# Orders of work at three places of a two-layer encoder kernel: the start, the scan scores, the entry of the odd layer

## The chip, the cores and the metric

The kernel runs on one core of a Trainium2 chip. The metric is the device time of one execution in microseconds (us); lower is better. The time before is the median of three runs, 1917.02 us (1916.12 to 1919.83). The engines are named as in the profile: PE is TensorE, PEld its weight load, DVE is VectorE, ACT is ScalarE, POOL is GpSimd, and SP issues transfers only.

## The reference

The input x has 256 positions (T) of 2048 channels, batch 1, fp32, and there are two layers. Layer 0 is even: one input projection feeds an SSD scan (centred width-5 convolution, chunks of 128, both directions) and a neighbourhood attention, and both go through one output projection. Layer 1 is odd: a convolution module with a GLU, a width-31 convolution and a layer norm. Behind each layer a gate adds a projected per-layer input p[i].

```python
def even_mixer(hn, w_in, ...):
    u = hn @ w_in
    z, xbc, dt_raw, q, k, v, g = jnp.split(u, ...)
    y_ssd = ssd_branch(z, xbc, dt_raw, ...)
    y_na = neighbourhood_attention(q, k, v, rpb) * jax.nn.silu(g)
    return jnp.concatenate([y_ssd, y_na], axis=-1) @ w_out

def conv_module(hn, w_in, dw_w, dw_b, ln_w, ln_b, w_out):
    a, a_gate, g = jnp.split(hn @ w_in, 3, axis=-1)
    v = a * jax.nn.sigmoid(a_gate)
    v = depthwise_conv(v, dw_w, dw_b)
    v = layernorm(v, ln_w, ln_b)
    v = jax.nn.silu(v) * jax.nn.silu(g)
    return v @ w_out

def per_layer_embedding(h, p_i, norm_w, w_gate, w_proj):
    gate = jax.nn.sigmoid(rmsnorm(h, norm_w) @ w_gate)
    return gate * (p_i @ w_proj)

h = x
for i in range(DEPTH):
    h = h + (even_mixer if i % 2 == 0 else conv_module)(rmsnorm(h, ...), ...)
    h = h + per_layer_embedding(h, p[i], ...)
return rmsnorm(h, final_norm_w)
```

In the scan of one group of four heads and one chunk, the scores are (C Bt) times exp(sum of decays) times dt; the kernel calls this product mT.

## The kernel before

**Projections.** Every fp32 projection is done in fp32r: each operand is split into a high part (a copy in fp32r) and a low part (the rest), and three matmuls per tile are summed: high by high, low by high, high by low. `proj` (L277-279) keeps the weights stationary and gives channels by positions; `proj_rows` (L305-307) keeps the activations stationary and gives positions by channels.

**Weights.** The class `Weights` cuts all weights into jobs of 512 KB, in the order in which they are used: two k tiles of 128 rows by 512 columns. For each job SP issues the load into `raw` (L96), ACT makes the high part `whi` (L99), and DVE, or POOL where a table says so, makes the low part `wlo` (L101). There are four buffers for raw and four for the parts. `fill(upto)` emits jobs up to a number, with high priority; `take()` hands the next job to a projection and keeps `AHEAD` = 3 jobs emitted ahead of it.

**Order.** PE runs in the order in which the program is written (`manual_schedule` for PE). On the other engines a scheduler orders the instructions; `tc.high_priority()` puts those inside it ahead of others that are ready. Small pieces of work are generators in the list `bg`: `pump(n)` takes n steps, and a projection calls it between two jobs. `wait(n)` is n empty steps, `drain()` runs all that is left.

**Normalization.** `TokNorm.feed(c)` squares a column block of h on ACT with a sum (L339, one instruction for each half a of the 256 positions); behind the fourth block DVE reduces the sums (L343, L344) and POOL takes the power -1/2 (L345), which gives `rh`. `scaled_blocks` multiplies h by it into `xs` (L418: a=0 on DVE, a=1 on POOL). `transposed` transposes xs on PE into `htp` (L407, two k tiles by four 128x128 transposes a step) and splits that with the norm weight into `ahi` on ACT (L319) and `alo` on DVE (L320), the operands of the next projection.

**The start.** ACT issues p[0] and four loads of x, one for each 512 columns of h (512 KB); POOL issues the first part of `vecs` (all small vectors); three weights are filled. p[0] is transposed and split (`load_p`, L317 for its low part), then the four blocks of h are squared, then four projections of p[0] run (`proj_rows`, four jobs). Their results are copied from PSUM into `ppb` (L432, a=0 on DVE, a=1 on ACT) and stored by POOL to DRAM as `pp0` for the gate. Then xs, two steps of transposes (`START_PAIRS` = 2) and the first big projection, `acc_b0`, of 512 columns. The other part of `vecs` (560 KB) is loaded by SP behind that projection's fill (L523).

**The scan.** Each group has PE build `seg`, the sums of decays, for both chunks (L588); ACT takes the Exp into mT (L593), and DVE multiplies it by dt (L594) and by the C B products (L595). A few jobs later PE multiplies mT with x into `ya` (L607). Between these, ACT and DVE do the width-5 convolution of the next channels: ACT the first tap and the Silu (L505 and L511), DVE four further taps (L509).

**The entry of the odd layer.** The gate of layer 0 (`gate`, with DVE at L765 and L766) adds to h and squares it. Behind it `load_p(1, ...)` issues the load of p[1], its two steps (`ptp`, L393, and split) run at once, then four `proj_rows` with p[1], copied by ACT (L784), then `scaled_blocks` into tiles of the pool `sg`, two steps of transposes, and the first GLU projection.

```python
    for c in range(NB):
        norm.feed(c)
...
    scaled_blocks(norm, xs)
    xn = []
    bg.append(transposed(xs, "ev_norm_w", xn))
    pump(START_PAIRS)
    acc_b0 = proj(LazyList(xn, KT), 512)
```

Of the kernel before, what the change touches and what calls it, by code (L numbers as in the profile page):

```python
# [44 lines left out]
START_PAIRS = 2  # L45
NB = D // 512
# [25 lines left out]
class Weights:  # L72


    def __init__(self, tc, pools, jobs):
# [6 lines left out]
        self.taken = 0  # L82

    def fill(self, upto):
        with self.tc.high_priority():
            while self.emitted < min(upto, len(self.jobs)):
                self.emit()

    def emit(self):
# [6 lines left out]
        nc.sync.dma_start(  # L96
            raw,
            w[k0 * P:(k0 + nk) * P, c0:c0 + ncols].rearrange("(k p) c -> p k c", p=P))
        nc.scalar.activation(hi, raw, AF.Copy)  # L99
        eng = nc.gpsimd if low(i) else nc.vector  # L100
        eng.tensor_sub(lo, raw, hi.bitcast(F32))  # L101
# [10 lines left out]
def trunk(ctx, tc, t, out, dbg=None):  # L112
# [201 lines left out]
    def split(hi, lo, src, scale=None, eng=None):  # L314
        if scale is None:
            nc.scalar.activation(hi, src, AF.Copy)
            (eng or nc.vector).tensor_sub(lo, src, hi.bitcast(F32))  # L317
        else:
            nc.scalar.activation(hi, src, AF.Copy, scale=scale)  # L319
            nc.vector.scalar_tensor_tensor(lo, src, scale, hi.bitcast(F32), op0=ALU.mult, op1=ALU.subtract)  # L320

    def operand(src, scale=None, where=None, eng=None):
        hi = (where or actp).tile([P, T], F32R, name="ahi", tag="ahi")
        lo = (where or actp).tile([P, T], F32R, name="alo", tag="alo")
        split(hi, lo, src, scale, eng)
# [3 lines left out]
    class TokNorm:  # L329


        def __init__(self):
            self.n, self.rstd = 0, None
# [45 lines left out]
    def load_p(i, pl_pool, pt=None):  # L379
# [6 lines left out]
        def steps():  # L386
          with tc.high_priority():
            for k in range(2):
# [5 lines left out]
                split(ph, pl, ps[:, :T])  # L394
                res.append((ph, pl))
                yield
# [15 lines left out]
    def scaled_blocks(norm, xs):  # L412

        with tc.high_priority():
            for c in range(NB):
                for a in range(2):
                    eng = nc.gpsimd if a else nc.vector
                    eng.tensor_scalar(xs[c][a], h[c][:, a, :], norm.rstd[:, a:a + 1], None, op0=ALU.mult)  # L418
# [4 lines left out]
    for _ in steps:  # L423
        pass
    norm = TokNorm()
    for c in range(NB):
        norm.feed(c)
    for c in range(NB):
        ppb = sp.tile([P, 2, 512], F32, name="ppb", tag="ppb")

        def ev_pp(a, acc):
            (nc.scalar.copy if a else nc.vector.tensor_copy)(ppb[:, a, :], acc)  # L432
        proj_rows(pk, ev_pp)
        nc.gpsimd.dma_start(pp_dram[c], ppb)
    xs = [[sp.tile([P, 512], F32, name="xs", tag="xs", bufs=2 * NB) for _ in range(2)] for _ in range(NB)]
    scaled_blocks(norm, xs)
    xn = []
    bg.append(transposed(xs, "ev_norm_w", xn))
    pump(START_PAIRS)
# [522 lines left out]
```

## Time and profile before

| | us |
|---|---|
| median of three runs | 1917.02 |
| the profiled execution, its own time | 1919.01 |
| its span in the trace | 1917.3 |
| mean granted PE clock over the span | 0.987 |
| loads of weights and inputs | 333.11 MB read, 176 GB/s over the span |

The first part of the profile's page gives the busy time of each engine, its fourth part the chain of work that ended last, by engine. A view by stretches gives the busy time of each engine between two points of time, and a list of waits says which operation on PE stood idle for which operation of another engine: its rows read "waiter <- releaser: sum of idle us, times, longest". A row of the timeline is the start of an operation (us from the span's start), its duration, engine, line, operation, tile out<-in, shapes, how many alike follow each other, and in brackets the idle time ahead and what ended it.

### The profile page before, as it was taken

To read this page: it belongs to the slowest core of one execution; us is meant where nothing else is said; L and a number is where in the kernel's file an instruction comes from. 1 tells how busy PE (TensorE), PEld (TensorE's weight loads), DVE (VectorE), ACT (ScalarE), POOL (GpSimd) and SP (SyncE) were. 2 spreads that over 40 slices of the span, in tenths; PEclk is the share of its full clock that TensorE was granted. 3 is DMA by queue.
4 is the path that set the end of the run, shared out by engine and by line. 5 is a ranking of instruction groups with operands and counts; after the bars stand their busy time and mean duration, and the time that the engine had idled before them with its cause. 6 is when DMAs were issued, how large, how long until landed. Compare 5 with 4: busy or idle time off the path is not lost.

```text
span 1917.3 us, 31565 instructions
## 1 busy us (share of the span) xinstructions
PE 1871.3 (98%) x12436; PEld 1723.2 (90%) x12436; DVE 1293.8 (67%) x2119; ACT 951.0 (50%) x1305; POOL 652.6 (34%) x393
## 2 busy tenths in 40 slices
PE   7999999999999999999999999999999999999997
PEld 5999898899999999888887999999999999888885
DVE  4778765664656566665555598888889959765564
ACT  4555554644444455544454544444445447544553
POOL 2002866640000000000000498888888855200011
PEclk8999999999999999999999999999999999999998
DMA  7656445456666666565555476666666655566553
GB/s 250 176 168 185 132 132 154 131 147 182 176 186 165 193 167 191 180 224 188 187 185 166 132 215 183 185 180 180 191 181 184 186 156 165 186 204 203 186 181 117
DMA packets 191189, 339.37 MB, mean 177 GB/s; under 512 B 25376, under 2 KB 34080, under 8 KB 190912
## 3 DMA queue, kind: packets, MB, share of 16 engines
q1 hardware_dynamic: 188480, 331.70, 58.0%
q10 hardware_dynamic: 1936, 3.41, 0.5%
q0 software_dynamic: 624, 2.24, 0.3%
q8 instruction: 97, 1.59, 0.3%
q14 instruction: 52, 0.43, 0.1%
HBM read 333.11 MB, written 4.19 MB: 176 GB/s over the span
## 4 chain that ended last, share of the span: by engine, by line
PE 89%; DVE 5%; issue 2%; DMA 1%; ACT 1%; POOL 1%; ACTq 0%; POOLq 0%; DVEq 0%; SPq 0%
PE acc L278 17%; PE acc L277 17%; PE acc L279 17%; PE acc L305 12%; PE acc L307 12%; PE acc L306 11%; DVE wlo L101 2%; ACT whi L99 1%; DVE xsg L509 1%; PE ya L607 1%; PE htp L407 1%; DVE vc L856 1%; PE seg L588 0%; DMA raw<-in_ev_w_in_dram 0%; DMA h<-in_x_dram 0%
## 5 line engine op out<-in xcount | busy, mean ns | idle before, releaser
L99 ACT ACTIVATE whi<-raw 128x1024 fp32r<-128x1024 f32 (+1 forms) x633 | 656.3, 1037 | 772.3 <-PE acc L278 374.0
L101 DVE TENSOR_TENSOR wlo<-raw,whi 128x1024 fp32r<-128x1024 f32 (+1 forms) x465 | 577.9, 1244 | 434.7 <-ACT whi L99 431.4
L277 PE MATMUL acc<-ahi,whi 128*128 128x256 f32 (+1 forms) x2832 | 806.6, 285 | 1.7 <-ACT ahi L319 1.7
L278 PE MATMUL acc<-alo,whi 128*128 128x256 f32 (+1 forms) x2832 | 803.2, 284 | 3.4 <-DVE alo L320 3.3
L279 PE MATMUL acc<-ahi,wlo 128*128 128x256 f32 (+1 forms) x2832 | 803.0, 284 | 2.0 <-DVE wlo L101 2.0
L278 PEld LDWEIGHTS acc<-alo,whi 128*128 128x128 f32 (+1 forms) x2832 | 543.4, 192 | 5.4 <-DVE alo L320 4.6
L277 PEld LDWEIGHTS acc<-ahi,whi 128*128 128x128 f32 (+1 forms) x2832 | 543.3, 192 | 3.4 <-ACT ahi L319 2.2
L279 PEld LDWEIGHTS acc<-ahi,wlo 128*128 128x128 f32 (+1 forms) x2832 | 543.3, 192 | 2.6 <-DVE wlo L101 2.6
L101 POOL TENSOR_TENSOR wlo<-raw,whi 128x1024 fp32r<-128x1024 f32 (+1 forms) x168 | 385.4, 2302 | 80.0 <-ACT whi L99 77.8
L305 PE MATMUL acc<-whi,ahi 128*128 128x512 f32 x1024 | 405.8, 396 | 2.5 <-DVE q4l L317 2.5
L307 PE MATMUL acc<-whi,alo 128*128 128x512 f32 x1024 | 402.5, 393 | 1.0 <-DVE alo L317 1.0
L306 PE MATMUL acc<-wlo,ahi 128*128 128x512 f32 x1024 | 402.2, 393 | 0.0
L822 DVE SCALAR_TENSOR_TENSOR cacc<-vc,vecs,cacc 128x249 f32<-128x249 f32 (+14 forms) x960 | 376.9, 472 | 8.1 <-ACT cacc L819 5.3
L345 POOL TENSOR_TENSOR rh<-rh,nhalf 128x2 f32<-128x2 f32 x5 | 3.5, 696 | 830.8 <-DVE rh L344 830.7
L307 PEld LDWEIGHTS acc<-whi,alo 128*128 128x128 f32 x1024 | 193.4, 189 | 44.3 <-DVE alo L317 1.4
L305 PEld LDWEIGHTS acc<-whi,ahi 128*128 128x128 f32 x1024 | 193.8, 189 | 43.6 <-DVE q4l L317 2.8
L306 PEld LDWEIGHTS acc<-wlo,ahi 128*128 128x128 f32 x1024 | 193.7, 189 | 40.7
L535 POOL TENSOR_SCALAR_AFFINE_SELECT dm<-dt_tok 128x512 f32<-128x512 f32 x32 | 32.3, 1013 | 140.2 <-DVE dt_tok L484 128.9
L319 ACT ACTIVATE ahi<-htp,vecs 128x256 fp32r<-128x256 f32 x64 | 29.3, 466 | 34.8 <-DVE alo L320 34.8
L809 DVE TENSOR_TENSOR vc<-acc,sg 128x512 f32<-128x512 f32 x16 | 11.1, 691 | 49.3 <-PE acc L279 49.0
L320 DVE SCALAR_TENSOR_TENSOR alo<-htp,vecs,ahi 128x256 fp32r<-128x256 f32 x64 | 30.3, 480 | 15.2 <-ACT ahi L319 15.2
L535 POOL TENSOR_SCALAR_AFFINE_SELECT segr<-ah 128x512 fp32r<-128x512 f32 x32 | 35.5, 1109 | 10.5 <-PE seg L588 10.2
(207 smaller groups left out, 1182.7 us busy)
## 6 DMA issues: line engine op xcount, KB each, us to landing
raw<-in_ev_w_in_dram SPq DMA_DIRECT2D x225, 512.0 KB, 3.7
raw<-in_od_w_in_dram SPq DMA_DIRECT2D x176, 512.0 KB, 4.3
raw<-in_ev_w_out_dram SPq DMA_DIRECT2D x64, 512.0 KB, 4.0
raw<-in_ple_w_gate_dram SPq DMA_DIRECT2D x64, 512.0 KB, 4.0
raw<-in_od_w_out_dram SPq DMA_DIRECT2D x64, 512.0 KB, 4.7
raw<-in_od_w_in_dram SPq DMA_DIRECT2D x32, 256.0 KB, 2.8
raw<-in_ple_w_proj_dram SPq DMA_DIRECT2D x8, 512.0 KB, 4.9
braw<-in_ev_rpb_dram SPq DMA_DIRECT2D x32, 96.0 KB, 6.9
```

Of the source, the lines that this page charges most:

```text
L99: nc.scalar.activation(hi, raw, AF.Copy)
L101: eng.tensor_sub(lo, raw, hi.bitcast(F32))
L277: nc.tensor.matmul(o, lhsT=hi[:, kk, cs], rhs=mh, start=st, stop=False, skip_group_check=True)
L278: nc.tensor.matmul(o, lhsT=hi[:, kk, cs], rhs=ml, start=False, stop=False, skip_group_check=True)
L279: nc.tensor.matmul(o, lhsT=lo[:, kk, cs], rhs=mh, start=False, stop=sp_, skip_group_check=True)
L305: nc.tensor.matmul(acc[c], lhsT=mh[:, ts_], rhs=hi[:, kk, :], start=k == 0, stop=False)
L306: nc.tensor.matmul(acc[c], lhsT=mh[:, ts_], rhs=lo[:, kk, :], start=False, stop=False)
L307: nc.tensor.matmul(acc[c], lhsT=ml[:, ts_], rhs=hi[:, kk, :], start=False, stop=k == nk - 1)
L319: nc.scalar.activation(hi, src, AF.Copy, scale=scale)
L320: nc.vector.scalar_tensor_tensor(lo, src, scale, hi.bitcast(F32), op0=ALU.mult, op1=ALU.subtract)
L535: nc.gpsimd.affine_select(out=out, in_=src[:, :, None].to_broadcast([P, 4, P]), pattern=[[0, 4], [pat, P]], compare_op=ALU.is_ge, fill=0.0 ...
L822: nc.vector.scalar_tensor_tensor(accs[b][:, c, lo_:hi_], av[b][:, c, lo_ + s:hi_ + s], w, accs[b][:, c, lo_:hi_], op0=ALU.mult, op1=ALU.add)
```

## The change

At the start, h becomes two tiles of 1024 columns, so x comes in two loads of 1 MB. One weight is filled ahead of the load of vecs. `behind()` holds back what is emitted inside it until the given instructions have been issued: the next three weights come behind the split of p[0]; the squares behind the split of the fourth weight; the fifth weight behind the last square and the first xs; and the further ones (up to the seventh) behind the last split of the first two transposing steps. Until then `W.limit` keeps `take()` from emitting more. The squares of a=1 go to DVE (an instruction that multiplies h by itself and sums), all copies to ppb to DVE with priority, with four buffers; of xs, POOL keeps a=1 of blocks 2 and 3, which holds in layer 1 too. The second part of vecs is loaded behind the last weight that was emitted by then.

In the scan, the Exp and the two products of mT get high priority. At the odd entry, p[1] is loaded ahead of the gate, and its two steps run within the gate's projections, behind two empty steps. The pools vc and sg are opened and xs is made ahead of the p[1] projections; the transposes may run within these, behind two empty steps, and two more steps follow them (`OD_PAIRS`).

```diff
@@ Weights
-            while self.emitted < min(upto, len(self.jobs)):
+            while self.emitted < min(upto, len(self.jobs), self.limit):
...
-        nc.sync.dma_start(
+        self.last = nc.sync.dma_start(
...
-        nc.scalar.activation(hi, raw, AF.Copy)
+        self.high = nc.scalar.activation(hi, raw, AF.Copy)
...
-        eng.tensor_sub(lo, raw, hi.bitcast(F32))
+        self.low = eng.tensor_sub(lo, raw, hi.bitcast(F32))
@@ trunk, first loads
-    h = [keep.tile([P, 2, 512], F32, name=f"h{c}") for c in range(NB)]
+    hx = [keep.tile([P, 2, 1024], F32, name=f"h{c}") for c in range(NB // 2)]
+    h = [hx[c // 2][:, :, c % 2 * 512:c % 2 * 512 + 512] for c in range(NB)]
...
-        for c in range(NB):
-            nc.scalar.dma_start(h[c], t["x"][0, :, 512 * c:512 * c + 512].rearrange("(a q) c -> q a c", q=P))
+        for c in range(NB // 2):
+            nc.scalar.dma_start(hx[c], t["x"][0, :, 1024 * c:1024 * c + 1024].rearrange("(a q) c -> q a c", q=P))
+        W.fill(1)
         nc.gpsimd.dma_start(vecs[:, :n0], t["vecs"][:, :n0])
-    W.fill(AHEAD)
@@ TokNorm
-        def feed(self, c):
+        def feed(self, c, both=False):
             for a in range(2):
                 junk = small.tile([P, 512], F32, name="junk", tag="sq", bufs=3)
-                nc.scalar.activation(junk, h[c][:, a, :], AF.Square, accum_out=self.ssq[:, a, c:c + 1])
+                if a and both:
+                    sq = nc.vector.scalar_tensor_tensor(junk, h[c][:, a, :], 1.0, h[c][:, a, :], op0=ALU.mult,
+                                                        op1=ALU.mult, accum_out=self.ssq[:, a, c:c + 1])
+                else:
+                    sq = nc.scalar.activation(junk, h[c][:, a, :], AF.Square, accum_out=self.ssq[:, a, c:c + 1])
+                self.last[a] = sq
@@ scaled_blocks
-                    eng = nc.gpsimd if a else nc.vector
-                    eng.tensor_scalar(xs[c][a], h[c][:, a, :], norm.rstd[:, a:a + 1], None, op0=ALU.mult)
+                    eng = nc.gpsimd if a and c > 1 else nc.vector
+                    i = eng.tensor_scalar(xs[c][a], h[c][:, a, :], norm.rstd[:, a:a + 1], None, op0=ALU.mult)
...
@@ trunk, start
-    for _ in steps:
-        pass
+    def behind(*insts):
+
+        st = ExitStack()
+        for x in insts:
+            st.enter_context(tc.issue_after(x.ins))
+        return st
+
+    last = list(steps)[-1]
+    with behind(*last):
+        W.fill(NB)
     norm = TokNorm()
+    with behind(W.high, W.low), tc.high_priority():
+        for c in range(NB):
+            norm.feed(c, both=True)
+    xs = [[sp.tile([P, 512], F32, name="xs", tag="xs", bufs=2 * NB) for _ in range(2)] for _ in range(NB)]
+    with behind(norm.last[0], scaled_blocks(norm, xs)):
+        W.fill(NB + 1)
+    W.limit = NB + 1
     for c in range(NB):
-        norm.feed(c)
-    for c in range(NB):
-        ppb = sp.tile([P, 2, 512], F32, name="ppb", tag="ppb")
+        ppb = sp.tile([P, 2, 512], F32, name="ppb", tag="ppb", bufs=NB)
 
         def ev_pp(a, acc):
-            (nc.scalar.copy if a else nc.vector.tensor_copy)(ppb[:, a, :], acc)
+            with tc.high_priority():
+                nc.vector.tensor_copy(ppb[:, a, :], acc)
...
     pump(START_PAIRS)
+    W.limit = len(W.jobs)
+    with behind(*halves):
+        W.fill(NB + AHEAD)
     acc_b0 = proj(LazyList(xn, KT), 512)
...
-    nc.sync.dma_start(vecs[:, n0:], t["vecs"][:, n0:])
+    with tc.issue_after(W.last.ins):
+        nc.sync.dma_start(vecs[:, n0:], t["vecs"][:, n0:])
@@ scan
-            nc.scalar.activation(m, seg, AF.Exp)
...
+            with tc.high_priority():
+                nc.scalar.activation(m, seg, AF.Exp)
+                nc.vector.tensor_tensor(m, m, dms[c], op=ALU.mult)
...
@@ entry of the odd layer
+    pk, steps = load_p(1, late)
+    bg.append(wait(2))
+    bg.append(steps)
     norm = gate(xg, norm.rstd, ppool)
     drain()
     s_xg.close()
-    pk, steps = load_p(1, ppool)
-    bg.append(steps)
-    pump(2)
+    s_p.close()
+    s_vc, cv = open_pool("vc", reuse_waits="tile")
...
+    scaled_blocks(norm, xs)
+    xn = []
+    bg.append(wait(2))
+    bg.append(transposed(xs, "od_norm_w", xn))
     for c in range(NB):
         def ev_pp(a, acc, c=c):
             nc.scalar.copy(ppt[c][:, a, :], acc)
         proj_rows(pk, ev_pp)
...
-    pump(START_PAIRS)
+    pump(OD_PAIRS)
```

**The start on DVE.** Before, behind the first weights of p[0] (wlo is a low part of a weight, ppb a copied result, xs a scaled block of h):

```order
L432 COPY ppb<-acc 128x512
L101 TENSOR_TENSOR wlo_240<-raw_238,whi_239 128x1024
L432 COPY ppb<-acc 128x512
L101 TENSOR_TENSOR wlo_264<-raw_262,whi_263 128x1024
L101 TENSOR_TENSOR wlo_288<-raw_286,whi_287 128x1024
L343 TENSOR_REDUCE rh<-ssq 128x2
L344 TENSOR_SCALAR rh<-rh 128x2
L459 TENSOR_SCALAR nega<-nega 64x1
L418 TENSOR_SCALAR xs<-h_85,rh 128x512
L418 TENSOR_SCALAR xs<-h_86,rh 128x512
L432 COPY ppb<-acc 128x512
L101 TENSOR_TENSOR wlo_353<-raw_351,whi_352 128x1024
```

After, at the same place, where junk is the square of a block and ssq its sum:

```order
L459 COPY ppb<-acc 128x512 x2
L102 TENSOR_TENSOR wlo_188<-raw_186,whi_187 128x1024
L459 COPY ppb<-acc 128x512 x2
L345 SCALAR_TENSOR_TENSOR junk,ssq<-h_85 128x512 x2
L459 COPY ppb<-acc 128x512 x2
L345 SCALAR_TENSOR_TENSOR junk,ssq<-h_86 128x512 x2
L459 COPY ppb<-acc 128x512 x2
L353 TENSOR_REDUCE rh<-ssq 128x2
L487 TENSOR_SCALAR nega<-nega 64x1
L354 TENSOR_SCALAR rh<-rh 128x2
L428 TENSOR_SCALAR xs<-h_85,rh 128x512 x3
```

The low parts of weights that belong to the first big projection have left the stretch ahead of rh; in their place stand four squares and all eight copies, and the first xs follow directly on rh.

**The scan on DVE.** Before, from a convolution (xsg) of a later channel group to the second chunk's products (mT):

```order
L101 TENSOR_TENSOR wlo_2505<-raw_2503,whi_2504 128x1024
L509 SCALAR_TENSOR_TENSOR xsg<-acc,vecs,xsg 128x255
L509 SCALAR_TENSOR_TENSOR xsg<-acc,vecs,xsg 128x254
L509 SCALAR_TENSOR_TENSOR xsg<-acc,vecs,xsg 128x255 x2
L509 SCALAR_TENSOR_TENSOR xsg<-acc,vecs,xsg 128x254
L509 SCALAR_TENSOR_TENSOR xsg<-acc,vecs,xsg 128x255
L101 TENSOR_TENSOR wlo_2530<-raw_2528,whi_2529 128x1024
L509 SCALAR_TENSOR_TENSOR xsg<-acc,vecs,xsg 128x254
L594 TENSOR_TENSOR mT<-mT,dm 128x512
L595 TENSOR_TENSOR mT<-mT,cbs 128x512
```

After, at the same place:

```order
L102 TENSOR_TENSOR wlo_2474<-raw_2472,whi_2473 128x1024
L537 SCALAR_TENSOR_TENSOR xsg<-acc,vecs,xsg 128x255 x2
L537 SCALAR_TENSOR_TENSOR xsg<-acc,vecs,xsg 128x254 x2
L537 SCALAR_TENSOR_TENSOR xsg<-acc,vecs,xsg 128x255
L102 TENSOR_TENSOR wlo_2501<-raw_2499,whi_2500 128x1024
L537 SCALAR_TENSOR_TENSOR xsg<-acc,vecs,xsg 128x255
L624 TENSOR_TENSOR mT<-mT,dm 128x512
L537 SCALAR_TENSOR_TENSOR xsg<-acc,vecs,xsg 128x254
L625 TENSOR_TENSOR mT<-mT,cbs 128x512
L102 TENSOR_TENSOR wlo_2526<-raw_2524,whi_2525 128x1024
```

The two products of the second chunk stood behind all 16 taps of that stretch and the weight ahead of the last tap; five and four taps now follow behind them instead of ahead, and so does one weight.

**The entry of the odd layer on ACT.** Before, behind the projections of p[1] (pp is a copied result of p[1], whi the high part of a weight, ahi a high part of a transposed operand):

```order
L784 COPY pp_8960<-acc 128x512
L99 ACTIVATE whi_10569<-raw_10568 128x512
L319 ACTIVATE ahi<-htp,vecs 128x256
L784 COPY pp_8960<-acc 128x512
L319 ACTIVATE ahi<-htp,vecs 128x256 x3
L99 ACTIVATE whi_10600<-raw_10599 128x512
L319 ACTIVATE ahi<-htp,vecs 128x256
L99 ACTIVATE whi_10631<-raw_10630 128x512
L319 ACTIVATE ahi<-htp,vecs 128x256 x3
L99 ACTIVATE whi_10662<-raw_10661 128x512
```

After, at the same place:

```order
L825 COPY pp_8955<-acc 128x512
L100 ACTIVATE whi_10530<-raw_10529 128x512
L321 ACTIVATE ahi<-htp,vecs 128x256
L825 COPY pp_8955<-acc 128x512
L321 ACTIVATE ahi<-htp,vecs 128x256
L825 COPY pp_8956<-acc 128x512
L100 ACTIVATE whi_10591<-raw_10590 128x512
L321 ACTIVATE ahi<-htp,vecs 128x256
L825 COPY pp_8956<-acc 128x512
L321 ACTIVATE ahi<-htp,vecs 128x256 x2
L100 ACTIVATE whi_10622<-raw_10621 128x512
L321 ACTIVATE ahi<-htp,vecs 128x256 x2
```

Before, the first operand came behind the third of the four pairs of copies and all others behind the last; now they begin two pairs of copies earlier and alternate with them.

More of the change, by code (lines that the diff above doesn't have):

```diff
@@ L45 @@
 START_PAIRS = 2
+OD_PAIRS = 2
 NB = D // 512
@@ L81, in __init__ @@
         self.emitted, self.ready = 0, []
-        self.taken = 0
+        self.taken, self.limit = 0, len(self.jobs)
     def fill(self, upto):
         with self.tc.high_priority():
-            while self.emitted < min(upto, len(self.jobs)):
+            while self.emitted < min(upto, len(self.jobs), self.limit):
                 self.emit()
@@ L324, in operand @@
         lo = (where or actp).tile([P, T], F32R, name="alo", tag="alo")
-        split(hi, lo, src, scale, eng)
+        halves[:] = split(hi, lo, src, scale, eng)
         return hi, lo
@@ L332, in __init__ @@
         def __init__(self):
-            self.n, self.rstd = 0, None
+            self.n, self.rstd, self.last = 0, None, [None, None]
             self.ssq = small.tile([P, 2, NB], F32, name="ssq", tag="ssq")
-        def feed(self, c):
+        def feed(self, c, both=False):
             for a in range(2):
                 junk = small.tile([P, 512], F32, name="junk", tag="sq", bufs=3)
-                nc.scalar.activation(junk, h[c][:, a, :], AF.Square, accum_out=self.ssq[:, a, c:c + 1])
+                if a and both:
[4 more added lines that the diff above has]
+                self.last[a] = sq
             self.n += 1
@@ L393, in steps @@
                     nc.tensor.transpose(ps[:, a * P:(a + 1) * P], pt[:, a, k * P:(k + 1) * P], ident)
-                split(ph, pl, ps[:, :T])
+                last = split(ph, pl, ps[:, :T])
                 res.append((ph, pl))
-                yield
+                yield last
         return res, steps()
@@ L592, in ssd_group @@
             m = sd.tile([P, 4, P], F32, name="mT", tag="mT")
-            nc.scalar.activation(m, seg, AF.Exp)
-            nc.vector.tensor_tensor(m, m, dms[c], op=ALU.mult)
-            nc.vector.tensor_tensor(m, m, cbs[:, c, None, c * P:(c + 1) * P].to_broadcast([P, 4, P]), op=ALU.mult)
+            with tc.high_priority():
+                nc.scalar.activation(m, seg, AF.Exp)
+                nc.vector.tensor_tensor(m, m, dms[c], op=ALU.mult)
+                nc.vector.tensor_tensor(m, m, cbs[:, c, None, c * P:(c + 1) * P].to_broadcast([P, 4, P]), op=ALU.mult)
             mts.append(m)
@@ L778, in trunk @@
     s_xg.close()
-    pk, steps = load_p(1, ppool)
-    bg.append(steps)
-    pump(2)
-    for c in range(NB):
-        def ev_pp(a, acc, c=c):
-            nc.scalar.copy(ppt[c][:, a, :], acc)
-        proj_rows(pk, ev_pp)
-    for c in range(NB):
-        dump(f"hB{c}", h[c])
     s_p.close()
@@ L797, in trunk, with ev_pp @@
     xn = []
+    bg.append(wait(2))
     bg.append(transposed(xs, "od_norm_w", xn))
-    pump(START_PAIRS)
+    for c in range(NB):
+        def ev_pp(a, acc, c=c):
+            nc.scalar.copy(ppt[c][:, a, :], acc)
+        proj_rows(pk, ev_pp)
+    for c in range(NB):
+        dump(f"hB{c}", h[c])
+    pump(OD_PAIRS)
     xn = LazyList(xn, KT)
```

15 lines of the change are left out of this document (9 added, 6 removed).

## The prediction

> **What bounds the kernel now.** I read the page's first and fourth part, then a table of busy time by stage, then the list of who waited for whom on TensorE (PE), and last the timeline where PE stood still.
>
> ```profile
> PE 1871.3 (98%) x12436; PEld 1723.2 (90%) x12436; DVE 1293.8 (67%) x2119; ACT 951.0 (50%) x1305; POOL 652.6 (34%) x393
> ...
> PE 89%; DVE 5%; issue 2%; DMA 1%; ACT 1%; POOL 1%; ACTq 0%; POOLq 0%; DVEq 0%; SPq 0%
> ```
> ```profile
> 0.00:33.00 33.00, 22.23 (x76) 16.61 (x77) 12.63 (x18) 15.75 (x32) 7.91 (x21) 0.79 0.83 281
> 33.00:65.00 32.00, 28.72 (x228) 28.29 (x226) 19.86 (x29) 17.24 (x28) 5.02 (x5) 0.95 0.54 168
> ...
> 180.00:430.00 250.00, 241.91 (x1594) 222.55 (x1592) 159.65 (x191) 130.57 (x196) 153.65 (x141) 0.98 0.49 143
> 430.00:1040.00 610.00, 608.97 (x3709) 545.51 (x3710) 355.93 (x448) 297.16 (x404) 0.69 (x1) 1.00 0.64 185
> 1040.00:1081.00 41.00, 37.38 (x219) 31.61 (x217) 25.27 (x43) 24.67 (x47) 7.77 (x5) 1.00 0.35 105
> ```
> ```profile
> PE ya L607 <- DVE mT L595: 6.3, 3, 2.1
> PE acc L305 <- DVE ppb L432: 5.4, 2, 3.6
> PE acc L278 <- DVE alo L320: 3.3, 5, 1.8
> ```
>
> PE is the bound: 98% busy, 89% of the chain. The change leaves its work alone, so only its 46 us of idle time (1917.3 - 1871.3) and what runs at a lower granted clock can be won. The stages (columns: stretch, length, then busy time of PE, PEld, DVE, ACT, POOL, granted clock, DMA share, GB/s) show where that lies: 10.8 us idle before 33 us at a clock of 0.79, 3.3 us to 65, 8.1 in the scan, 3.6 around 1060. The change touches just these; from 430 to 1040 only 1.0 of 610 us is idle.
>
> **First place, the start.**
>
> ```profile
> 14.62 1.06 ACT L99 ACTIVATE whi<-raw 128x1024 fp32r<-128x1024 f32 x1 [1.63 <-DMA raw<-in_ple_w_proj_dram]
> ...
> 15.71 1.23 DVE L101 TENSOR_TENSOR wlo<-raw,whi 128x1024 fp32r<-128x1024 f32 x1 [1.46 <-ACT whi L99]
> ...
> 16.85 0.68 DVE L432 COPY ppb<-acc 128x512 f32<-128x512 f32 x1
> ...
> 22.25 0.80 PE L305 MATMUL acc<-whi,ph 128*128 128x512 f32 x1 [3.56 <-DVE ppb L432]
> ...
> 28.42 0.17 DVE L344 TENSOR_SCALAR rh<-rh 128x2 f32<-128x2 f32 x1
> ...
> 29.84 1.63 DVE L418 TENSOR_SCALAR xs<-h,rh 128x512 f32<-128x512 f32 x2 [0.94 <-POOL rh L345]
> ...
> 36.80 0.47 DVE L320 SCALAR_TENSOR_TENSOR alo<-htp,vecs,ahi 128x256 fp32r<-128x256 f32 x1
> ```
> ```profile
> 37.33 0.39 PE L278 MATMUL acc<-alo,whi 128*128 128x256 f32 x1 [1.82 <-DVE alo L320]
> ...
> 58.30 0.60 PE L407 MATMUL htp<-ident,xs 128*128 128x128 f32 x4
> ```
> ```profile
> wf<-in_final_norm_w_dram SPq DMA_DIRECT2D x1, 1024.0 KB, 6.6
> ```
> ```profile
> DMA to landing us min/median/max: 8.7/10.4/12.5
> ```
> ```profile
> 1048.56 0.69 DVE L765 TENSOR_TENSOR gate<-gate,pp 128x512 f32<-128x512 f32 x1 [0.50 <-ACT gate L764]
> ```
>
> Before, PE stands between the four small projections of p0, because ACT and DVE copy and square in turns with weights of a later projection (3.56 us before 22.25). What counts is when the first big projection gets its first low operand: 37.33, which waits for alo at 36.80. That projection then runs to about 64.4 (the last transposes at 58.30, 0.36 until the next matmul, two jobs of 2.87).
>
> After: the fourth p0 weight is split as before (high part 14.62, low part done by 16.9), since the four loads keep their place on SP's queue. PE needs each 2.74 us per projection (12 matmuls at 0.228) and ends p0 near 21. DVE is later: from 16.9 two copies (0.65 each, by 0.68), two squares, two copies, two squares, two copies, all in order. A square on DVE reads h twice and also gives a sum; no row shows it. Between 0.61 (a square's ACT time) and twice the 0.69 of the two-input row, I take 0.75, near that row. So 16.9 + 6 x 0.65 + 4 x 0.75 = 23.8. Reduce, nega and rh take 0.45; from rh to xs took 1.25 (28.59 to 29.84), POOL's power among it: 25.5. POOL now issues all four stores of pp ahead of that power; the last waits for the last copy, 23.8, and its 0.6 fits before 24.25. Three xs at 0.8 (1.63 for two), one low weight 1.2, two xs at 0.6, and alo: 25.5 + 2.4 + 1.2 + 1.2 + 0.5 = 30.8. That is **6.5 earlier**. DVE has 6 xs instead of 4, POOL 2 instead of 4; the last is behind the first alo and so hidden.
>
> Given back: the second, third and fourth weight of the big projection are now split only from about 32.5 (ACT has four ahi first), and the sixth raw buffer comes free at about 35, so that load lands at 38.8 (3.7 us, the page's median) while ACT holds the operands of the third job behind it. I charge one wait of 1.2. **Start: 6.5 - 1.2 = 5.3 us.** The big load of vecs leaves the start and comes behind the eleventh weight of that projection; it may hold one weight by some 3 us, which the four buffers cover (a job is 2.87, a load 3.7).
>
> The unknown is x in two loads of 1 MB instead of four of 512 KB. The same bytes on the same queue landed 8.7 to 12.5 after issue; a 1 MB load elsewhere took 6.6. The second one is issued at 6.0 as before, behind the first high weight. Bounds: 6.6 to 25 (twice 12.5), landing 12.6 to 31. I take 12.5, nearest to those rows: 18.5, before DVE squares it at 21. At 31, everything behind waits 10 us.
>
> [...]
>
> **Second place, the scan.**
>
> ```profile
> 206.91 1.89 PE L607 MATMUL ya<-xtk,mT 128*128 128x64 f32 x16
> ...
> 208.61 0.36 PE L277 MATMUL acc<-ahi,whi 128*128 128x256 f32 x1
> ```
> ```profile
> 221.83 1.28 ACT L511 ACT_TABLE_LOAD   x1 [4.01 <-DVE xsg L509]
> ...
> 227.97 0.60 ACT L593 ACTIVATE mT<-seg 128x512 f32<-128x512 f32 x1
> ```
> ```profile
> 232.30 0.69 DVE L595 TENSOR_TENSOR mT<-mT,cbs 128x512 f32<-128x512 f32 x1
> ```
> ```profile
> 229.90 1.00 PE L607 MATMUL ya<-xtk,mT 128*128 128x64 f32 x8
> 233.05 1.63 PE L607 MATMUL ya<-xtk,mT 128*128 128x64 f32 x8 [2.15 <-DVE mT L595]
> 234.44 0.77 PE L305 MATMUL acc<-whi,ahi 128*128 128x512 f32 x1
> ...
> 237.03 0.40 PE L305 MATMUL acc<-whi,ahi 128*128 128x512 f32 x1
> ```
>
> In three of eight groups the second eight ya matmuls wait for mT. Eight take 0.85 when nothing is late (16 in 1.70, 206.91 to 208.61), so they could start at 230.75 and end at 231.6; the six matmuls behind would take 1.37 and the next start at 232.97. It starts at 237.03: the loss is **4.1 us**, not 2.15, since the ya and the six behind run slow. The two others lose about the same (2.07 idle each): 12.1.
>
> After, on DVE the first chunk's products come four convolution taps earlier, the second's five and four taps and one weight earlier; on ACT the second Exp no longer follows two of the four weights. From 218.34, DVE's order with the row times (tap 0.40, weight 1.2 to 1.5, product 0.6 to 0.85) ends the fourth tap at 222.75; ACT then loads its table (1.28), does the Silu, a first tap, a weight and the Exp's table, and Exp ends at 227.8, 0.7 sooner than before. DVE reaches the product at 228.3 and ends both at 230.0, against a need at 230.75. So the wait goes, **12.1 us**, with 0.7 to spare. What is late next: the weight behind (high part on ACT at about 230.4, low at 231.6), needed at 237.1. The bounds: none won (0) to all 12.1.
>
> [...]
>
> **Third place, p1 and the first GLU projection.**
>
> ```profile
> 1048.34 0.60 PE L393 MATMUL ptp<-ident,pt 128*128 128x128 f32 x4
> ...
> 1051.84 0.39 PE L305 MATMUL acc<-whi,ph 128*128 128x512 f32 x1
> ...
> 1062.16 1.04 PE L407 MATMUL htp<-ident,sg 128*128 128x128 f32 x8
> ...
> 1069.74 0.39 PE L278 MATMUL acc<-alo,whi 128*128 128x256 f32 x1 [0.37 <-DVE alo L320]
> ...
> 1079.44 0.28 PE L277 MATMUL acc<-ahi,whi 128*128 128x256 f32 x1
> ```
>
> The transposes of p1 and the split stand open: from 1048.34 to the fourth matmul 1051.84 are 3.50, where 0.44 + 3 x 0.228 = 1.13 would do. In the gate the same four transposes, two high and two low parts lie under 610 us of dense PE work, and the load of p1 stays on SP's queue long before them. **2.4 us.** Then from 1062.16 to the last job at 1079.44 and its 1.44: 18.7 us, where 8 transposes (0.88), 96 matmuls at 0.12 (11.5) and six pairs of transposes at 0.47 (2.8) are 15.2: **3.5 us** of short waits for operands (0.37 at 1069.74 is one). After, four steps of transposes lead instead of two, the first under the p1 projections. Its xs must be there when the third ends, 8.2 us after the gate; the chain gate, square, rstd, six xs puts the first two at about 7. Working the queues through, a pair of operands then costs ACT 1.45 and DVE 1.5 with its weight, PE 1.9 with transposes and 1.44 without; the lead of four lasts to the end. So **5.9 us** here; bounds 2.4 (the ring still limits) to 5.9. POOL keeps two of its four xs, DVE takes two more.
>
> **Sum.** 5.3 + 12.1 + 5.9 = 23.3 off the profiled execution's 1919.0 gives 1895.7. That execution lies 2.0 over the median of the three runs, 1917.0, so the forecast is 1893.7, say **1894**.
>
> **Rivals.**
> - *The scan's wait stays in part.* If POOL's products or slow weights on DVE hold the second product 1 us more, PE waits a little and its clock falls all the same; of 12.1 about 4 are left: 1902. For: only 0.7 to spare, and DVE and POOL disturb each other there. Against: five groups with another order wait not at all. 0.13.
> - *The start gains nothing*: x lands late (at 24 to 31) and PE waits as before: 1899 to 1904. For: 8.7 to 12.5 for half the size. Against: less is in flight without vecs. 0.12.
> [...]
> [...]
> - *The third place does not change its limit*: 1897, 0.05.
> - *Slower*: in the scan ACT and DVE are tied in a ring. The taps now stand behind the first product, the Silu's table waits for the taps (4.01 us in the row above), the second Exp for that, and DVE stands on it with weights behind. If the second product is x late, three groups lose x + 1.2 each; over 3.8 us slower than before from x = 8.2, and 1923 at x = 9. Against: it is worked out 0.7 early. 0.03.
>
> **How the numbers follow.** The forecast, 1890 to 1897, has 0.61; a bit better, 1886 to 1890 (a product or clock gain I undercount), 0.03; the rest as above. The range that leaves out under 2 in 10 and takes in the bounds of the loads and the scan is 1888 to 1904. A measurement of this kernel tells about 0.2%, 3.8 us, from no change: faster than 1913.2 is every case but the last and a small one where scan and start both fail: 0.94; within 0.2%: 0.03; slower: 0.03.
>
> **What would show it.** In the profile after: first alo matmul of the big projection near 31 and its end near 59; no idle time before p0's second to fourth projection; squares on DVE near 0.75; no wait of ya for mT and no slow matmuls near 232; ptp within the gate without a gap; the first GLU projection in about 15 us after its transposes. A landing of the second x load past 21, a wait of PE for wlo in the scan, or a clock under 0.95 there would make it wrong.

## The result and the profile after

The changed kernel takes **1895.55 us** (median of 4, 1894.52 to 1897.74) against 1917.53 us of before in the same comparison: a ratio of 0.9885, 95% interval 0.9873 to 0.9897, or 22.0 us. The forecast was 1894. The profiled execution took 1894.52 us, its span is 1892.8, its mean granted clock 0.993; it is 24.5 shorter than that of before.

The page of after, its first and fourth part:

```profile
PE 1858.0 (98%) x12436; PEld 1714.2 (91%) x12436; DVE 1305.3 (69%) x2135; ACT 945.0 (50%) x1293; POOL 650.3 (34%) x389
...
PE 90%; DVE 5%; issue 2%; ACT 1%; POOL 1%; DMA 1%; SPq 0%; POOLq 0%; ACTq 0%; DVEq 0%
```

The same matmuls (12436) are busy for 13.3 us less, since fewer of them run at a low clock; idle time falls from 46.0 to 34.8. Busy time by stage of after (columns: stretch, length, busy PE, PEld, DVE, ACT, POOL, granted clock, DMA share, GB/s):

```profile
0.00:28.00 28.00, 18.41 (x75) 14.34 (x76) 14.78 (x30) 10.07 (x19) 7.90 (x22) 0.94 0.87 314
28.00:58.00 30.00, 27.97 (x214) 27.36 (x213) 21.05 (x31) 16.95 (x26) 2.98 (x2) 0.89 0.60 190
...
180.00:415.00 235.00, 231.81 (x1571) 214.30 (x1569) 164.12 (x189) 128.08 (x195) 156.28 (x141) 1.00 0.50 147
415.00:1024.00 609.00, 608.41 (x3716) 544.97 (x3717) 355.79 (x450) 297.66 (x406) 0.69 (x1) 1.00 0.63 186
1024.00:1058.00 34.00, 34.00 (x212) 30.16 (x211) 24.87 (x43) 23.50 (x46) 4.95 (x3) 1.00 0.40 119
```

The start granted 0.94 instead of 0.79 (but the stretch behind it 0.89 instead of 0.95), the scan 1.00 instead of 0.98 with 3.2 us idle instead of 8.1, and the entry of the odd layer has no idle time left. The list of PE's waits of after:

```profile
PE htp L417 <- DVE xs L428: 4.6, 2, 4.2
...
PE acc L280 <- DVE alo L322: 2.0, 2, 1.3
...
PE acc L307 <- DVE ppb L459: 1.8, 1, 1.8
...
PE ya L637 <- DVE mT L625: 0.9, 3, 0.4
```

The waits of ya for mT fell from 6.3 to 0.9 but not to nothing. At the start PE now stands mainly in one piece ahead of the first transposes (4.2); of the three waits for copies between the projections of p0 one is left (1.8).

To see where 24.5 us went, each profile is cut at four events on its timeline: the last transposes of the start, the first matmul of the value projection (it waits for q4l, the low part of the first split of q), the first score matmul (sps), and the first Sigmoid of the GLU. Between two events the work is the same in all kernels, but for the constant matmuls that fill_before, fill9_before and combined add. Lengths in us:

| kernel | to last transposes | to value projection | to first sps | to first Sigmoid |
|---|---|---|---|---|
| before | 58.30 | 372.4 | 49.4 | 601.4 |
| after | 52.98 | 362.3 | 47.8 | 595.4 |
| start_only | 53.57 | 370.8 | 49.4 | 601.3 |
| scan_only | 58.77 | 362.3 | 47.8 | 603.0 |
| odd_only | 56.72 | 370.8 | 49.4 | 595.4 |
| fill_before | 59.89 | 372.7 | 49.4 | 603.1 |
| fill9_before | 60.09 | 367.8 | 47.9 | 602.9 |
| scan_exp | 53.03 | 360.7 | 49.4 | 595.4 |
| start_sq_act | 52.57 | 362.2 | 47.8 | 595.4 |
| start_nohold | 58.45 | 362.3 | 49.4 | 595.4 |
| start_x4 | 51.56 | 362.3 | 47.8 | 595.4 |
| odd_p1 | 52.82 | 362.4 | 49.4 | 599.3 |
| best | 52.13 | 362.4 | 49.4 | 596.4 |
| combined | 49.72 | 362.4 | 47.8 | 595.4 |

Start 5.3, scan 10.1, entry 6.0: these are the three places, 21.5 us in sum. The other 3.0 lie where the change does nothing: 1.6 in the third column, and 1.4 behind the Sigmoid. The rows show what the third column is. Before, around the first matmuls of the value projection:

```profile
430.73 0.50 PE L305 MATMUL acc<-whi,ahi 128*128 128x512 f32 x1 [2.53 <-DVE q4l L317]
...
432.88 0.63 PE L305 MATMUL acc<-whi,ahi 128*128 128x512 f32 x1
433.30 0.63 PE L306 MATMUL acc<-wlo,ahi 128*128 128x512 f32 x1
```

After, the same place:

```profile
415.28 0.50 PE L307 MATMUL acc<-whi,ahi 128*128 128x512 f32 x1 [2.53 <-DVE q4l L319]
...
417.45 0.39 PE L307 MATMUL acc<-whi,ahi 128*128 128x512 f32 x1
417.68 0.39 PE L308 MATMUL acc<-wlo,ahi 128*128 128x512 f32 x1
```

The gap is 2.53 us in both. Before, the matmuls behind it start 0.42 apart (432.88 to 433.30); after, 0.23. Behind the one gap the clock fell, behind the other it didn't, and that is worth 1.6 us. This sets the two profiles apart by chance; the medians, 22.0, hold less of it. Behind the Sigmoid it is the gap ahead of the layer norm's sums (tile ss), 2.54 in before and 2.56 in after: the clock fell behind both, but from the first ss to the tile rps behind them before took 7.86 us and after 6.26.

The fourth column holds such chance too. scan_only, fill_before and fill9_before have the entry of before, yet they show 602.9 to 603.1 where before and start_only show 601.3 to 601.4. Rows of scan_only at the entry:

```profile
1040.29 0.50 PE L307 MATMUL acc<-whi,pl 128*128 128x512 f32 x1 [0.85 <-DVE pl L317]
...
1041.47 0.63 PE L305 MATMUL acc<-whi,ph 128*128 128x512 f32 x1
1041.89 0.63 PE L306 MATMUL acc<-wlo,ph 128*128 128x512 f32 x1
```

In before the same waits, 0.98 for ph and 0.84 for pl, were followed by matmuls at full clock (0.23 apart, from 1051.84 on). So the entry's 6.0 is measured against the better case of before; against the other three profiles it is 7.5 to 7.7.

### The profile page after: what moved, and what is told of

The parts are those of the page before. It is cut to its first block, busy times and chain, and to the rows that moved or that the text cites. A ratio compares the mean times of both kernels' runs of the same rounds, so it can differ in the third digit from the quotient of the medians.

```text
span 1892.8 us, 31552 instructions
## 1 busy us (share of the span) xinstructions
PE 1858.0 (98%) x12436; PEld 1714.2 (91%) x12436; DVE 1305.3 (69%) x2135; ACT 945.0 (50%) x1293; POOL 650.3 (34%) x389
## 4 chain that ended last, share of the span: by engine, by line
PE 90%; DVE 5%; issue 2%; ACT 1%; POOL 1%; DMA 1%; SPq 0%; POOLq 0%; ACTq 0%; DVEq 0%
PE acc L280 17%; PE acc L279 17%; PE acc L281 17%; PE acc L307 12%; PE acc L309 12%; PE acc L308 11%; DVE wlo L102 2%; PE htp L417 1%; DMA raw<-in_ple_w_proj_dram 1%; DVE xsg L537 1%; PE ya L637 1%; DVE vc L886 1%; PE seg L617 0%; ACT whi L100 0%; DVE lnsq L892 0%
```

## The experiments

All times are medians against the kernel before on the same chip; the columns of the table above belong to the profile of each. The expectations name the value projection's gap and its 1.6 us where it matters.

### Each place alone

**start_only** has the first place alone (POOL's share of xs changed at the start only).

> Before with the first place alone (the start; the scan and the entry of the odd layer as before, and POOL's share of xs changed at the start only). Theory A, the three places add up and what PE gains at the start stays gained: the last transposes of the start come 5.3 us earlier, as between the profiles of before and after (58.30 to 52.98), and the time is 1917.5 - 5.3 = 1912.2. Rival B, the start's gain is given back later unless the scan is mended too (weights run short in the scan): 1917.5, with longer waits of ya for mT. The two gaps on PE that the change doesn't touch (2.5 us ahead of the value projection, and the layer norm) may each be followed by slow matmuls or not, 1.6 us either way.

Measured: ratio 0.9975 (0.9966 to 0.9985), 4.8 us of 1920.0. The last transposes came 4.7 earlier, and the scan kept its three waits (6.3 in sum). Theory A; what PE gains at the start isn't given back in the scan.

**scan_only** has only the priority:

```diff
-            nc.scalar.activation(m, seg, AF.Exp)
-            nc.vector.tensor_tensor(m, m, dms[c], op=ALU.mult)
+            with tc.high_priority():
+                nc.scalar.activation(m, seg, AF.Exp)
+                nc.vector.tensor_tensor(m, m, dms[c], op=ALU.mult)
...
```

> Before with the second place alone (priority for the Exp and the two products of mT). Theory A: each of three groups gains 3.4 us as between the two profiles (5.32 to 15.45 over the three), 10.1 in all: 1907.4, with waits of ya for mT of 0.3 to 0.4. Rival B, a good part of it came from the other two places (their shift changed how loads and the scan meet): under 6 us, 1912 or more.

Measured: 0.9951 (0.9937 to 0.9965), 9.4 us; the scan stage is 362.3 as in after. Theory A.

**odd_only** has only the entry of the odd layer.

> Before with the third place alone (p1 loaded and split during the gate, scaling and transposes ahead; POOL's share of xs changed there only). Theory A: 6.0 us, from the first sps to the first Sigmoid of the GLU: 1911.5. Rival B, the entry is then held by a ring of other operands and only the split of p1 counts: 2.4 us, 1915.1.

Measured: 0.9967 (0.9956 to 0.9979), 6.3 us; the stage is 595.4 as in after. Theory A. The three alone make 0.25 + 0.49 + 0.33 = 1.07%, all together 1.15% (1.03 to 1.27): they add up.

### How much of a gap is clock: fill_before and fill9_before

Both are the kernel before, with matmuls of a constant in the gaps of the scan, 18 a group in fill_before and 9 in fill9_before:

```diff
         for c in range(2):
+            if c and g in (1, 3, 5):
+                for _ in range(9):
+                    nc.tensor.matmul(ya[:, 1, 0:P], lhsT=ones, rhs=ones, start=True, stop=True)
             for hd in range(4):
```

> Before, with 18 matmuls of a constant by itself on PE ahead of the second eight ya matmuls of the three groups that wait for mT (their result is overwritten). They fill the wait of 2.1 us with work and bring mT no earlier. Theory A, of the 3.4 us that a group loses some 2.1 are the wait and 1.3 to 1.5 the lower granted clock behind it: with the gap filled the six matmuls behind run in 1.4 instead of 2.6, the granted clock stays at 1.00, and the time is 1917.5 - 3 x 1.4 = 1913.3. Rival B, the slow matmuls come from the operands or PSUM and not from the gap: they stay slow, 1917.5 to 1918. Rival C, the filling itself delays ya (18 at 0.11 are 2.0): 1918 to 1919.

Measured: 1.000 (0.9991 to 1.0009). In its profile, each such matmul appears as two records, and 18 take 4.1 us, not 2.0: they overshoot the gap by 2.0, yet the time is unchanged, since the matmuls behind ran at full clock in all three groups (1.00 granted from 229 to 240, around the first). Theories A and C both, cancelling; so the size was mended:

> Before, with 9 instead of 18 matmuls of a constant ahead of the second eight ya matmuls of the three groups (18 took 4.1 us where the wait was 2.1, so 9 should take 2.05). mT comes no earlier. Theory A, of the 3.4 us per group a part is the lower granted clock behind the gap, 1.25 us where it falls (it fell behind 7 of 9 such gaps in the profiles of before, of the start alone and of the entry alone): the wait is filled, no group has slow matmuls, and the time is about 3 x 0.97 = 2.9 below before, 0.15%. Rival B, the slow matmuls have another cause and stay: no change. The matmuls filled in change nothing of the result.

Measured: 0.9977 (0.9968 to 0.9986), 4.4 us **faster than before, with mT no earlier**. Rows of fill9_before at the first of the three groups:

```profile
231.69 1.00 PE L610 MATMUL ya<-xtk,mT 128*128 128x64 f32 x8
232.53 2.23 PE L608 MATMUL ya<-ones 128*128 128x128 f32 x18
234.84 1.10 PE L610 MATMUL ya<-xtk,mT 128*128 128x64 f32 x8
235.75 0.48 PE L305 MATMUL acc<-whi,ahi 128*128 128x512 f32 x1
...
237.22 0.40 PE L305 MATMUL acc<-whi,ahi 128*128 128x512 f32 x1
```

The six matmuls behind take 1.47 (235.75 to 237.22) instead of 2.59 (234.44 to 237.03). The stage is 4.6 shorter than in the profile of before, 1.5 a group. So of the 3.4 us that the change won per group there, about 1.5 were the clock behind the gap and 1.9 the gap. But the clock doesn't always fall. In start_only, behind the same gap:

```profile
228.31 1.10 PE L636 MATMUL ya<-xtk,mT 128*128 128x64 f32 x8 [2.13 <-DVE mT L624]
229.23 0.48 PE L307 MATMUL acc<-whi,ahi 128*128 128x512 f32 x1
...
230.69 0.39 PE L307 MATMUL acc<-whi,ahi 128*128 128x512 f32 x1
```

Here the six take 1.46. Over the profiles of before, start_only and odd_only it fell behind 7 of 9 such gaps of 2.06 to 2.15.

### Which part of the scan's edit counts: scan_exp

```diff
             with tc.high_priority():
                 nc.scalar.activation(m, seg, AF.Exp)
-                nc.vector.tensor_tensor(m, m, dms[c], op=ALU.mult)
+            nc.vector.tensor_tensor(m, m, dms[c], op=ALU.mult)
...
```

> After, with the priority in the scan on the Exp alone, not on the two products. In DVE's order the second chunk's products stay where they are (behind the same eight taps since the first chunk's second product and two weights), and the first chunk's come four taps later. Theory A, what counts is the second chunk's place on DVE, which the Exp's place on ACT sets: 1895.5, waits of ya for mT of 0.3 to 0.4 still. Rival B, the products' own priority does it: waits of about 2.1 in three groups as before, 1895.5 + 10.1 = 1905.6, or a part of it.

Measured: 0.9882 (0.9867 to 0.9897), as after. Theory A, and better than expected: no ya waits at all. Rows of scan_exp:

```profile
224.63 1.90 PE L637 MATMUL ya<-xtk,mT 128*128 128x64 f32 x16
226.34 0.48 PE L307 MATMUL acc<-whi,ahi 128*128 128x512 f32 x1
```

All sixteen run in a row, and the stage is 1.6 shorter than in after. With the products' priority the first chunk's products go ahead of four taps; the Silu's table load then comes 1.24 later (216.56 here, 217.80 in after), the second Exp 0.29 (221.94, 222.23), and the second chunk's last product 0.49 (224.47, 224.96). In this profile the clock fell behind the gap ahead of the value projection, so that its span doesn't show the gain, nor does the interval. Priority on the products alone was not run, so whether it would do as well as the Exp's is not shown.

### Parts of the start

**start_sq_act**: `norm.feed(c)` instead of `norm.feed(c, both=True)`, all squares on ACT.

> After, with all eight squares of the start on ACT, none on DVE. ACT does them from 17.3 at 0.63 each with one weight among them, the last ends near 23.4; DVE is free of four at 0.61 and gets to the sum of squares near 23.5 instead of 24.7, but two copies then stand among the first xs. Theory A, DVE is the chain of the start and the squares on it cost: the first low operand comes 0.6 earlier (30.2), the time is 1895. Rival B, ACT becomes the chain and the squares on DVE pay: first low operand 1 later or more, 1896.5 or more.

Measured: 0.9878 (0.9865 to 0.9892); first low operand's matmul at 29.93 (after: 30.82), last transposes 0.4 earlier. Theory A by the profile: the squares on DVE win nothing, they cost a little; the times alone can't tell it from no change.

**start_nohold**: `behind()`, the limit and the priority of the squares taken out, the rest of the start kept.

```diff
-    with behind(*last):
-        W.fill(NB)
+    W.fill(AHEAD)
...
-    with behind(W.high, W.low), tc.high_priority():
-        for c in range(NB):
-            norm.feed(c, both=True)
+    for c in range(NB):
+        norm.feed(c, both=True)
...
```

> After without the holding back at the start: weights are filled three ahead as before, squares have no priority, and the limit is gone; squares of a=1 and all copies stay on DVE. DVE then has four low parts of weights of the big projection (1.22 each) ahead of or among squares and copies; worked out by its order the sum of squares comes near 29.9 instead of 24.7, the first low operand near 36 instead of 30.8. Theory A, the gain of the start is the holding back of the weights: it is nearly all lost, 1895.5 + 4.5 = 1900. Rival B, it is the copies and squares on DVE: the first low operand stays under 32, 1896.

Measured: 0.9903 (0.9889 to 0.9916), 1900.66. Its sum of squares and first low operand:

```profile
31.24 0.16 DVE L353 TENSOR_REDUCE rh<-ssq 128x2 f32<-128x8 f32 x1
```
```profile
36.63 0.58 PE L280 MATMUL acc<-alo,whi 128*128 128x256 f32 x1 [0.70 <-DVE alo L322]
```

Theory A: last transposes at 58.45, as before the change. Without holding back the weights of the big projection (and the squares' priority, which went with it) nothing is left of the gain of the start; the copies and squares on DVE alone bring none of it. Holding back with the copies shared as before was not run.

**start_x4**: x in four loads of 512 KB, as before the change.

```diff
-        for c in range(NB // 2):
-            nc.scalar.dma_start(hx[c], t["x"][0, :, 1024 * c:1024 * c + 1024].rearrange("(a q) c -> q a c", q=P))
+        for c in range(NB):
+            nc.scalar.dma_start(h[c], t["x"][0, :, 512 * c:512 * c + 512].rearrange("(a q) c -> q a c", q=P))
```

> After, with x in four loads of 512 KB instead of two of 1 MB. Theory A, the landing of x isn't on the chain of the start (the squares wait for the split of the fourth weight): the first low operand stays at 30.8 within 0.5, and so does the time, 1895.5. Rival B, the two large loads are what lets x be there: the last squares wait, first low operand 1 to 3 later, 1896.5 to 1898.5.

Measured: 1893.12 (2 runs), 0.9873 (0.9853 to 0.9893). Neither theory: the first low operand came 1.8 **earlier**. The high part of the fourth p0 weight, on ACT, in start_x4:

```profile
14.59 1.06 ACT L100 ACTIVATE whi<-raw 128x1024 fp32r<-128x1024 f32 x1 [1.65 <-DMA raw<-in_ple_w_proj_dram]
```

In after:

```profile
16.21 1.06 ACT L100 ACTIVATE whi<-raw 128x1024 fp32r<-128x1024 f32 x1 [1.11 <-DMA raw<-in_ple_w_proj_dram]
```

With two loads of 1 MB on ACT's queue the p0 weights on SP's queue come 1.6 us later, and the start hangs on those weights, not on x. The DMA view of the first 12 us shows the share that moved: ACT's queue (q10) carried 1.83 MB in after and 1.39 in start_x4, SP's queue (q1) 1.52 and 1.83. It repeats: over the seven profiles with four loads (before among them) this instruction starts at 14.59 to 14.90, over six with two at 16.18 to 16.29. (In start_nohold, with two loads too, it is 13.66; there the second load of x was issued only at 10.16, in after at 6.19.)

### Parts of the entry: odd_p1

p1 is split in the gate, but the scaling and the transposes follow the p1 projections, as before the change.

```diff
-    scaled_blocks(norm, xs)
-    xn = []
-    bg.append(wait(2))
-    bg.append(transposed(xs, "od_norm_w", xn))
     for c in range(NB):
         def ev_pp(a, acc, c=c):
...
+    scaled_blocks(norm, xs)
+    xn = []
+    bg.append(transposed(xs, "od_norm_w", xn))
     pump(OD_PAIRS)
```

> After, but with the scaling and the transposes of h behind the projections of p1, as before; p1 is still loaded and split during the gate. Theory A, the two parts of the entry add up: the split of p1 in the gate is worth 2.4 us, the scaling and transposes ahead 3.6, and this loses the second: 1895.5 + 3.6 = 1899.1. Rival B, the split alone brings nothing once the operands come late: 1901.5. Rival C, the split was all of it: 1895.5.

Measured: 1898.42, 0.9900 (0.9884 to 0.9917). The stage is 599.3: of 6.0 us the split is 2.1 and the lead of transposes 3.9 (the 2.1 against before's own profile; where the clock fell behind the split's waits it is 3.6 to 3.8). Theory A. The ring of operands is back, as a wait of 0.37 at every other pair of operands. Two of its four rows in odd_p1:

```profile
1046.59 0.38 PE L280 MATMUL acc<-alo,whi 128*128 128x256 f32 x1 [0.37 <-DVE alo L322]
...
1052.12 0.39 PE L280 MATMUL acc<-alo,whi 128*128 128x256 f32 x1 [0.37 <-DVE alo L322]
```

### Two attempts at a better kernel

**best** and **combined** are after with further edits at the start and ahead of the value projection. The core of best:

```diff
+            with ExitStack() as st:
+                if c < ahead:
+                    st.enter_context(tc.high_priority())
                 for a in range(2):
                     eng = nc.gpsimd if a and c > 1 else nc.vector
...
-            finish(q_acc, ev_q)
+            with tc.high_priority():
+                finish(q_acc, ev_q)
             finish(k_acc, ev_k)
```

> After with two further edits: at the start only the first block of xs has priority, so the first low operand follows the first weight instead of three more xs (it should start near 29.3 instead of 30.3); and the first two splits of q in the attention have priority, ahead of two copies of 0.41 on ACT, so that the gap of 2.5 us ahead of the value projection shrinks to about 1.7. Theory A: 1.3 at the start, 0.8 at the gap and on average 1 of clock behind it: 1892.5. Rival B, the start's part is given back since the second to fourth weight are split no earlier: 1894.

Measured: 1897.44, 0.9896 (0.9882 to 0.9911): not better than after. The start kept 0.85 of the 1.3. The split of q came earlier on ACT, but its low part then stood behind a weight on DVE, the gap stayed at 2.45, and the clock fell behind it in this profile (49.4). And the entry of the odd layer took 1.0 more: the priority was opened once for each block instead of once for all, and DVE now does its six scalings there in one row (from 1038.59) instead of three and three. In combined, which opens it once there, the stage is 595.4 again.

combined has the edits of start_x4 and start_sq_act, the scaling in two groups (the first block with priority, the others without) at the start alone, and

```diff
             finish(k_acc, ev_k)
+            ps = ms.tile([P, P], F32, name="warm", tag="ms")
+            for _ in range(9):
+                nc.tensor.matmul(ps, lhsT=ones, rhs=ones, start=True, stop=True)
```

> After with four edits: x in four loads of 512 KB (alone it brought the transposes of the start from 52.98 to 51.56), all squares of the start on ACT (52.57 alone), only the first block of xs ahead of the first weight (52.13 together with another edit), and 9 matmuls of a constant on PE in the gap of 2.5 us ahead of the value projection (2.05 us of work, so that the granted clock doesn't fall behind it; it fell by about 1.6 us in half of the profiles). The instructions of the other stages keep the order of after. Theory A, the three at the start add up to 2.7 us (last transposes at 50.3) and the fourth is worth 0.8 on average: 1895.5 - 3.5 = 1892.0. Rival B, the start's three meet the same limit (the first weights' split and the copies on DVE), 1.4 to 1.8 in all: 1893.0. The matmuls filled in change nothing of the result.

Measured: **1891.35** (1890.76 to 1893.74), 0.9862 (0.9845 to 0.9878): the lowest of all medians, 4.2 under after. The intervals of the two ratios overlap (after: 0.9873 to 0.9897), so that it beats after is shown by the stage, not by the times alone. The last transposes of the start are 3.3 earlier than in after, and the gap ahead of the value projection:

```profile
412.12 0.50 PE L306 MATMUL acc<-whi,ahi 128*128 128x512 f32 x1 [0.52 <-DVE q4l L318]
```

Theory A for the start. Whether the filled gap is worth 0.8 on average is not shown by this run: in after's own profile the clock hadn't fallen there.

## Why the prediction was right

**The start**, forecast 5.3, measured 5.3 (58.30 to 52.98). Its two parts: first low operand 6.5 earlier, measured 6.51 (37.33 to 30.82); 1.2 given back, measured 1.2 (from there to the last transposes 20.97 before, 22.16 after). That both agree so closely is in part luck. Inside the first part two errors cancelled. The fourth p0 weight was taken as split at 14.62, as before; it was 16.21, and start_x4 shows that the large x loads did it. That x lands late was weighed in the prediction; that its loads hold up the weights was not. On the other side DVE was faster than priced. After's squares, copies and scalings:

```profile
19.81 0.68 DVE L345 SCALAR_TENSOR_TENSOR junk<-h 128x512 f32<-128x512 f32 x1
...
20.42 0.69 DVE L345 SCALAR_TENSOR_TENSOR junk<-h 128x512 f32<-128x512 f32 x1
...
24.66 0.15 DVE L353 TENSOR_REDUCE rh<-ssq 128x2 f32<-128x8 f32 x1
...
26.39 1.71 DVE L428 TENSOR_SCALAR xs<-h,rh 128x512 f32<-128x512 f32 x3 [1.37 <-POOL rh L355]
```

A square follows another after 0.61, not 0.75; three xs take 1.71, not 2.4. So xs began 0.9 later than forecast (26.39 instead of 25.5), and what follows took 0.9 less.

In the second part the wait that was charged is there, for an operand behind a weight that ACT splits first (at 38.87), but it is 0.70 instead of 1.2:

```profile
41.64 0.39 PE L280 MATMUL acc<-alo,whi 128*128 128x256 f32 x1 [0.70 <-DVE alo L322]
```

The other 0.5 is clock: behind the first low operand the matmuls start 0.21 apart instead of 0.12 for about 4 us in after and about 3 in before. In odd_only, whose start is that of before, none ran slow there and the stretch took 19.41. Over the five profiles with that start the last transposes come at 56.72 to 60.09, over the four with the start of after at 52.82 to 53.57.

**The scan**, forecast 12.1, measured 10.1: the mechanism was right, but a small wait stayed that the forecast took to be gone. The step by which eight ya take 0.85 and the six behind them 1.37, so that each group loses 4.1, put the seventh matmul behind ya 3.07 after the first ya; after's rows give 3.75:

```profile
224.58 1.00 PE L637 MATMUL ya<-xtk,mT 128*128 128x64 f32 x8
225.94 1.10 PE L637 MATMUL ya<-xtk,mT 128*128 128x64 f32 x8 [0.36 <-DVE mT L625]
...
228.33 0.40 PE L307 MATMUL acc<-whi,ahi 128*128 128x512 f32 x1
```

In scan_exp, where nothing waits, it is 3.18 (224.63 to 227.81), so that step was right to 0.1. The rest is the step "DVE reaches the product at 228.3 and ends both at 230.0, against a need at 230.75": the product came 0.36 late instead of 0.7 early, in three groups. Moved to the time of after (5.3 earlier) the Exp was forecast to end at 222.5 and DVE to begin the products at 223.0; measured are 222.83 and 223.92, with a weight and a tap on DVE between. That is the ring of the "slower" rival at a small size, as scan_exp shows. Beside that small margin the prediction names that DVE and POOL disturb each other there: in before, from 65 to 430, a low part of a weight on DVE took 1.22 on average (1.15 to 1.23, 66 of them) with POOL idle, and 1.51 (1.21 to 1.99, 35 of them) with POOL busy for over half of it; POOL's selects (L535, 128x512) took 0.63 with DVE idle, 1.08 on average (0.63 to 1.62) with DVE busy for over half. Against a before whose clock falls behind two of three gaps, the stage is worth 8.5 (370.8 to 362.3).

**The entry**, forecast 5.9 (2.4 and 3.5), measured 6.0 (2.1 and 3.9). The mechanism is that of the forecast: in after no wait is left there, and odd_p1 divides the two parts. That the sum fits so well rests on before's profile, where the clock held behind the waits of the split; this chance was in no term.

**What the sum left out.** The forecast took the profile of before as the usual case and subtracted its offset from the median. That profile had the clock fall behind every gap of 2 us and more (2.07 to 3.56), but not behind the shorter waits at the odd entry (0.98 and 0.84). Gaps of 2.06 to 2.53 did cost the clock, so the prediction was right to charge it, but it took the fall for certain, where it came behind 7 of 9 of those at 2.06 to 2.15. Of the 24.5 us between the two profiles 3.0 are such chance, and were in no term; of the 23.3 that were forecast, the medians gave 22.0, and the scan's term, 2.0 too large, is the one that falls short.

## What to carry to other kernels

Where an engine works through two streams at a tight start, hold back the stream that isn't due: here that, with the squares' priority, brought the last transposes from 58.45 to 52.98, more than moving work between engines, which alone brought none of it. A larger load on one queue can delay the small ones on another that the start hangs on: with two loads of 1 MB instead of four of 512 KB the p0 weights came 1.6 us later. A gap on PE can cost more than its length, since the clock can fall behind it: of the 3.4 us won per group in the scan about 1.5 were clock, and it fell behind 7 of 9 such gaps. So count the matmuls behind it too, and compare medians, or stages over several profiles, not two single ones, for gains of a few us. If the wait can't go, work without use can fill it: nine matmuls of a constant in each of three gaps won 4.4 us.

## What the runs showed of the hardware

The fall of the granted clock behind a gap is not set by the program alone. In odd_p1 and after, which are the same program up to there, the value projection starts at 415.25 and 415.28 behind the same gap of 2.53; in odd_p1 the clock fell (the matmuls behind come to start 0.42 apart), in after not (0.23). Over 13 profiles with that gap (2.45 to 2.53) it fell in 8, the stage being 49.4 long, and not in 5, at 47.8 to 47.9. Shorter waits can do it too: behind the 0.98 and 0.85 at the old entry it fell in 3 of 5 profiles. What decides whether it falls isn't shown here. A matmul of the constant takes 0.227 us (18 in 4.08, from 232.31 to 236.39 in fill_before).
